# Token-major projections as products of 512 columns, and norms spread by transfers over DRAM

## The chip, the cores and the metric

The kernel runs on one core of one Trainium2 chip. The metric is the device time of one execution in microseconds (us); the kernel before takes 1825.83 us, the median of 3 runs (1825.49 to 1829.49).

## The reference

One inference step of an encoder layer. 2048 prompt tokens and 8 sample sequences of 16 tokens, each a row x of 1024, are RMS-normalised and multiplied by one weight matrix; the columns of the result feed three groups of heads, whose gated outputs go through an output projection.

```python
h = rms_norm(x, norm_g) @ w_in
fox_cols, rwkv_cols, mem_cols = jnp.split(h, [FOX_COLS, FOX_COLS + RWKV_COLS], axis=-1)
# fox: q, k (normalised per head of 64), v, forget gates; causal attention with a decay bias
# memory: q (normalised per head), attention into 256 memory tokens
# rwkv: r, k, v, decay, a, gate; per head and token
kk = k * ph(k_k)
kk = kk * lax.rsqrt(jnp.maximum(jnp.sum(kk * kk, axis=-1, keepdims=True), 1e-24))
S, y = rwkv_scan(s0, r, decay, k, v, kk, a)
mu = jnp.mean(y, axis=-1, keepdims=True)
var = jnp.mean(jnp.square(y - mu), axis=-1, keepdims=True)
yn = (y - mu) * lax.rsqrt(var + GN_EPS) * ph(gn_w) + ph(gn_b)
...
y = x + o @ w_out
```

Here rwkv has 6 heads of 64, fox 6 and memory 4. All is fp32. Two norms matter for the change: that of `kk` and that of `yn`, each one number per head and token, which then multiplies all 64 channels of the head.

## The kernel before

**Two stages.** The first stage (`p1`, to about 1130 us) normalises x, makes all projections and the whole rwkv group; what the attention needs goes to DRAM (`q_d`, `k_d`, `v_d`, `mq_d`, gates `fg_d`, `mg_d`, outputs `o_d`). The second stage (`p2`) does the attentions and the output projection. Buffers of the second stage lie where those of the first were, so a first buffer of `lt` (attention weights `P`, the raw output weights) is free only when the first stage's last user of that memory is done.

**Products in three parts.** The matrix engine takes fp32 data rounded to a shorter form (fp32r in the profile). x and each weight block are split into a high and a low part; a product is high x high + high x low + low x high. The contraction of 1024 goes in 8 blocks k of 128. x lies channel-major, `xk[k]` is 128 channels x (high, low) x up to 640 tokens. `wd_load` brings 256 weight columns into two tiles `hl` (4 blocks of k each, `[part, k, column]`): in the first of four iterations from the input, splitting them on ScalarE and GpSimd and keeping the split form in DRAM (`w_d`); in the other three from there, 1 MB at a time.

**Channel-major and token-major.** `proj_d` (tile `pjd`) makes channel-major results: the weights are stationary, 256, 384 or 512 tokens stream. `wide` (tile `pjt`) makes token-major results of 128 tokens x 256 columns: x is stationary and the weights stream, three products of 256 columns for each k. One PSUM tile `pjt` holds two token tiles side by side, 48 products. PSUM tiles `pjt`, `pjd` and a few others share the 3 buffers of `pj`. `put` then copies the pair of token tiles to SBUF on ScalarE (tile `qk`, 2 buffers), normalises the heads of q and k (square on ScalarE, sum on VectorE, power on GpSimd, multiply on VectorE, gain on GpSimd) and stores them. Five `wide` sets over 17 token tiles, and two sets over the two tiles of the memory, make 89 token tiles.

**rwkv.** Per iteration (512 prompt tokens) and pair of heads p: `rwkv_in` prepares, and solves small triangular systems, whose blocks go to DRAM and back (`ld`, `yt`, `xd`); `rwkv_mid` and `rwkv_scan` run the chunks; `rwkv_out` normalises and gates, and stores to `o_d`. The samples are three more such passes of 128 tokens. In `rwkv_in` and `rwkv_out`, `per_head` sums squares over a head's 64 channels with tiny products (tile `pss`) into `inv`, tokens on partitions, one column per head and tile of 128 tokens; then `spread` brings those numbers back to channel-major form, each repeated over 64 partitions: for each column one fp32 product, stationary the column repeated 64 times, streaming the identity (tile `spr`). VectorE multiplies straight from PSUM: into `ar[:, 0]` in `rwkv_in`, into `ysb` (tile `yd`) in `rwkv_out`.

**The order.** All DMAs are issued by SyncE (its queue is SPq). The program is emitted in a natural order; then `_arrange` re-orders all of it: `_Op` gives each instruction a cost, `_schedule` simulates the five engines with buffers and waits, 18 tries are made, and the try with the shortest simulated end becomes the order of every engine. An engine takes its instructions strictly in that order. For a DMA the planner has four terms: SyncE's own time, a lag to the transfer's begin (300 ns), the time on the wire, and a time to landing.

Of the kernel before, what the change touches and what calls it, by code (L numbers as in the profile page):

```python
# [9 lines left out]
F32 = mybir.dt.float32  # L10
# [7 lines left out]
KC = 8  # L18
# [33 lines left out]
def kernel(ctx: ExitStack, tc: tile.TileContext, I: dict, O: dict):  # L52
    nc = tc.nc
    V, S, G, PE, SY = nc.vector, nc.scalar, nc.gpsimd, nc.tensor, nc.sync
# [3 lines left out]
    def mm(out, lhsT, rhs, start=True, stop=True):  # L58
        PE.matmul(out, lhsT, rhs, start=start, stop=stop, skip_group_check=True)  # L59

    def tt(e, out, a, b, op):
        e.tensor_tensor(out=out, in0=a, in1=b, op=op)  # L62

    def stt(out, a, s, b, op0, op1):
        V.scalar_tensor_tensor(out=out, in0=a, scalar=s, in1=b, op0=op0, op1=op1)
# [9 lines left out]
    M, A_, SUB, MAX = ALU.mult, ALU.add, ALU.subtract, ALU.max  # L75
# [47 lines left out]
    with ExitStack() as p1:  # L123
# [48 lines left out]
        def wd_load(*parts, src="w_in"):  # L172


            where, n = [], 0
            for c0, w in parts:
                if where and where[-1][0] + where[-1][1] == c0:
                    where[-1][1] += w
                else:
                    where.append([c0, w, n])  # L180
                n += w
            key = (src, *parts)
            kept = split.get(key)
            if kept is None and src == "w_in":
                split[key] = dt(f"w{len(split)}_d", [256, 8 * n])
            hl = [[], []]
            for j, k0 in enumerate(range(0, KC, 4)):
                both = ws.tile([128, 2, 4, 256], F32R, tag="hl", name="w")
                flat = both.rearrange("p a k c -> p (a k c)")[:, :8 * n]
                hi, lo = (flat[:, 4 * n * a:4 * n * (a + 1)].rearrange("p (k c) -> p k c", c=n) for a in range(2))  # L190
                if kept is not None:
                    SY.dma_start(flat.bitcast(F32), kept[128 * j:128 * j + 128])
                else:
                    raw = ws.tile([128, 4, 256], F32, tag="w", name="wraw", bufs=WRAW)[:, :, :n]
                    for c0, w, o in where:
                        SY.dma_start(raw[:, :, o:o + w], I[src][128 * k0:128 * (k0 + 4), c0:c0 + w].rearrange("(k p) c -> p k c", p=128))
                    S.copy(hi, raw)  # L197
                    tt(G, lo, raw, hi.bitcast(F32), SUB)
                    if key in split:
                        SY.dma_start(split[key][128 * j:128 * j + 128], flat.bitcast(F32))  # L200
                hl[0].append(hi)
                hl[1].append(lo)
            return hl

        def proj_d(hl, c, m, xk, off, n):
# [132 lines left out]
        def at(h, a=0):  # L338

            return slice(64 * (h ^ a), 64 * (h ^ a) + 64)  # L340

        def per_head(sq, nt):

            pss = ps.tile([128, 512], F32, tag="ra", name="pss")
            for t in range(nt):
                for j in range(2):
                    mm(pss[64 * j:64 * j + 64, 2 * t:2 * t + 2], sq[:, 128 * t + 64 * j:128 * t + 64 * j + 64],
                       bones[:, 0:128:64].bitcast(F32))
            r = sm.tile([128, 8], F32, tag="inv", name="inv")[:, :2 * nt]
            V.tensor_copy(r, pss[:, :2 * nt])  # L350
            return r

        def spread(r, nt, pool, tag):

            out = pool.tile([128, 512], F32, tag=tag, name="spr")
            for t in range(nt):
                for h in range(2):
                    mm(out[at(h), 128 * t:128 * t + 128], r[:, 2 * t + h:2 * t + h + 1].to_broadcast([128, 64]), ident)
            return out[:, :128 * nt]

        def rwkv_in(p, k, r, v, g, sample, tok0):

# [34 lines left out]
            V.tensor_copy(wc, wx[:, :, seg])  # L397

            stt(seg3(ar[:, 0, :n]), seg3(k), col(NKK), wx[:, :, 0:seg], M, M)
            tt(V, ar[:, 0, :n], ar[:, 0, :n], spread(inv, nt, ps, "ra"), M)  # L400
            tt(V, seg3(ar[:, 1, :n]), seg3(r), wx[:, :, 1:seg + 1], M)

            ts(G, e5, e3, col(HKA), col(OHKA), M, A_)
# [233 lines left out]
        def rwkv_out(p, sample, n, nch, tok0, gt, bv, py, so):  # L637

            nt = n // 128
            two = rv.tile([128, 2, 512], F32, tag="bt", name="yd")  # L640
            ysb, sq = two[:, 0, :n], two[:, 1, :n]
            S.copy(ysb, py.rearrange("p c t -> p (c t)")[:, :n])
            yc = pg.tile([128, 512], F32, tag="gr", bufs=2, name="yc")[:, :n]
            mm(yc, centre, ysb)
            S.activation(sq, yc, AF.Square)
            S.copy(ysb, yc)
            r = per_head(sq, nt)
            rsqrt_small(r, r, 2 * nt, 1.0 / 64, GN_EPS)
            stt(ysb, ysb, vh[:, GW5 + p:GW5 + p + 1], spread(r, nt, ps, "ra"), M, M)
            stt(bv, bv, vh[:, GB5 + p:GB5 + p + 1], ysb, A_, A_)  # L650
            tt(V, bv, bv, gt, M)
            SY.dma_start(o_d[384 + 128 * p:384 + 128 * (p + 1), tok0:tok0 + n], bv)
            if sample:
                for c in range(2):
                    pt = pg.tile([128, 512], F32, tag="gr", bufs=2, name="pst")
                    for s in range(4):
                        PE.transpose(pt[0:64, 128 * s:128 * s + 128], so[:, c, s, :], ident)
                    sst = rv.tile([64, 4, 2, 64], F32, tag="gm", name="sst", bufs=2)
                    S.copy(sst, pt[0:64, :].rearrange("p (s h k) -> p s h k", h=2, k=64))
                    for h in range(2):  # L660
                        SY.dma_start(O["rs_s"][4 * c:4 * c + 4, 2 * p + h].rearrange("s v k -> v s k"), sst[:, :, h, :])
# [39 lines left out]
                tt(G, o_[:, :, n * j:n * j + n], s4[:, :, n * j:n * j + n],  # L701
                   GAIN[w].unsqueeze(1).unsqueeze(1).to_broadcast([128, nt, n, 64]), M)

        def put(out, parts, t0):

            nt, n = out.shape[1], len(parts)
            o_ = sm.tile([128, 512], F32, tag="qk", name="qk")[:, :128 * nt * n].rearrange("p (t c) -> p t c", t=nt)
            h4 = lambda ap: ap.rearrange("p t (h d) -> p t h d", d=64)
            whats = [w for w, _ in parts]
            S.copy(o_, out)  # L710
            n = sum(GAIN[w] is not None for w in whats)
            if n:
                normed(h4(o_[:, :, :128 * n]), whats[:n])
            spans_ = [(0, 2, parts[0])] if len(parts) == 2 and parts[1] == (whats[0], parts[0][1] + 128) else [
                (j, 1, x) for j, x in enumerate(parts)]
            for j, m, (w, c) in spans_:
                for dst in targets(w, t0, nt):
                    SY.dma_start(dst[:, :, c:c + 128 * m], o_[:, :, 128 * j:128 * (j + m)])
# [5 lines left out]
        def wide(parts, xk, nt, t0):  # L724
            hl = wd_load(*columns(parts), src="w_mem" if parts[0][0] in "KV" else "w_in")
            for a in range(0, nt, 2):
                m = min(2, nt - a)
                out = pj.tile([128, 2, 256], F32, tag="pj", name="pjt")
                for t in range(m):
                    ts_ = slice(128 * (a + t), 128 * (a + t) + 128)  # L730
                    for k in range(KC):
                        for x, y in ((0, 0), (0, 1), (1, 0)):
                            mm(out[:, t], xk[k][:, x, ts_], hl[y][k // 4][:, k % 4],
                               start=k == 0 and x + y == 0, stop=k == KC - 1 and x == 1)
                put(out[:, :m], parts, 16 if a == 4 else t0 + a)

        def narrow(hl, c, part, xk, blocks, tok0):

# [6 lines left out]
        def turn(sb, off, nb, part, tok0):  # L745
            pt = pj.tile([128, 512], F32, tag="pj", name="ptok")
            for t in range(nb // 128):
                PE.transpose(pt[:, 128 * t:128 * t + 128], sb[:, 128 * t:128 * t + 128], ident)
            for a, m, r0 in spans(tok0, off, nb):
                put(pt[:, a:a + m].rearrange("p (t c) -> p t c", c=128), [part], r0 // 128)  # L750

        def gate(hl, c, dst, xk, blocks, tok0):
            for off, nb in blocks:
# [179 lines left out]
    with ExitStack() as p2:  # L933
# [497 lines left out]
        at, mix = 0, []  # L1431
# [112 lines left out]
class _Op:  # L1544


    def __init__(self, i, eng):
# [25 lines left out]
        if eng == "SP":  # L1573
            size = 4 * list(outs[0].ap)[0][1] * _free(list(outs[0].ap))
            run = min(4 * list(a.ap)[-1][1] if list(a.ap)[-1][0] == 1 else 4 for a in aps)
            self.own, self.wire = (430 if run < 512 else 360), size / 230
            self.time = 1300 + (size / 140 - size / 230) * (run < 1024) / 2
            return
        wide = sum(k > 1 and "SB" in space(a) for k, a in zip(sizes, ins))
        self.reads = wide > 0  # L1580
# [201 lines left out]
def _schedule(p, rank, stay, loose=()):  # L1782
# [33 lines left out]
    while len(order) < count:  # L1816
# [37 lines left out]
        c = cost[nodes[x][0]]  # L1854
        if e == "SP":
            free[e] = s + c.own
            wire = max(wire, s + c.own + 300) + c.wire
            end[x] = wire + c.time
        elif e == "PE":
            for j, k in enumerate(nodes[x]):  # L1860
# [168 lines left out]
```

## Time and profile before

| | |
|---|---|
| median of 3 runs | 1825.83 us (1825.49 to 1829.49) |
| profiled execution, its own time | 1826.43 us |
| its span | 1824.6 us |
| TensorE matmul (PE) busy | 1756.1 us, 96% |
| VectorE (DVE), ScalarE (ACT), GpSimd (POOL) busy | 927.2, 895.5, 793.7 us |
| mean granted TensorE clock | 0.967 |

The profile names a group of instructions by the tile written, the tiles read (for a matmul the streaming one first, then the stationary one), its shape and its count. The two times of a timeline row are the start and the length of a run of like instructions, in us from the span's start. A matmul's recorded duration has a fixed tail that overlaps the next one; how fast they follow is read from the length of a run over its count. In the waits, the first column is who waited, then for whom, the total, the times, the longest.

### The profile page before, as it was taken

What the parts mean: (1) busy time and instruction counts of PE and PEld (TensorE: products, weight loads), DVE (VectorE), ACT (ScalarE), POOL (GpSimd) and SP (SyncE); (2) the same over time, 40 slices, a digit from 0 to 9 for tenths busy, and PEclk for the clock granted to TensorE, in tenths of its full rate; (3) what the DMA queues carried; (4) which work ended last, traced back from release to release, by engine and by line L of the source; (5) the groups of instructions that cost most, each with busy time, mean ns of one, the idle gap of its engine ahead of it and who ended that gap; (6) DMA issues with size and microseconds to landing.
All of it is one profiled execution on the core that took longest, in us unless ns stands there. A gap on an engine that the chain in (4) does not pass through costs nothing.

```text
span 1824.6 us, 41978 instructions
## 1 busy us (share of the span) xinstructions
PE 1756.1 (96%) x16883; PEld 1395.2 (76%) x16883; DVE 927.2 (51%) x2102; ACT 895.5 (49%) x1755; POOL 793.7 (43%) x818
## 2 busy tenths in 40 slices
PE   7999999999999999998999998999999999999998
PEld 6998999788877888876788886666666566667776
DVE  5544444464445553545743453767455545575213
ACT  5424343524234323324332434887888477986452
POOL 4555342242131341311332152567676265876452
PEclk8999999999999999999999999899999589999999
DMA  6767463745446464535363353434437542354422
GB/s 193 242 206 242 138 203 113 240 164 174 139 153 203 148 220 163 161 102 178 108 220 131 124 156 120 155 117 156 152 124 242 181 160 87 124 174 145 159 99 97
DMA packets 208905, 292.42 MB, mean 160 GB/s; under 512 B 56844, under 2 KB 161790, under 8 KB 192838
## 3 DMA queue, kind: packets, MB, share of 16 engines
q1 hardware_dynamic: 208710, 289.73, 48.5%
q8 instruction: 133, 2.18, 0.5%
q14 instruction: 62, 0.51, 0.1%
HBM read 202.58 MB, written 87.08 MB: 159 GB/s over the span
## 4 chain that ended last, share of the span: by engine, by line
PE 79%; DVE 7%; ACT 5%; DMA 3%; issue 3%; SPq 1%; POOL 1%; DVEq 0%; ACTq 0%; POOLq 0%
PE pjd L59 20%; PE pjt L59 12%; PE py L59 10%; PE po L59 9%; PE pS L59 7%; PE pm L59 4%; PE sc L59 2%; PE sy L59 1%; PE gr L59 1%; PE pz L59 1%; PE pa L59 1%; PE spr L59 1%; DMA w<-w_d 1%; PE gw L59 1%; PE gx L59 1%
## 5 line engine op out<-in xcount | busy, mean ns | idle before, releaser
L59 PE MATMUL pjd<-xk,w 128*128 128x512 f32 (+4 forms) x2280 | 522.6, 373 | 8.9 <-DVE xk L62 4.1
L59 PEld LDWEIGHTS pjd<-xk,w 128*128 128x128 f32 (+1 forms) x2280 | 380.4, 190 | 75.6 <-issue 10.2
L62 POOL TENSOR_TENSOR Pl<-P,Ph 128x512 fp32r<-128x512 f32 (+3 forms) x272 | 315.4, 1170 | 158.5 <-ACT Ph L1137 122.2
L59 PE MATMUL pjt<-w,xk 128*128 128x256 f32 x2040 | 282.4, 290 | 6.8 <-issue 3.5
L59 PEld LDWEIGHTS pjt<-w,xk 128*128 128x128 f32 x2040 | 260.1, 193 | 16.0 <-issue 7.8
L59 PE MATMUL py<-W,oh 128*128 128x512 f32 x816 | 248.7, 404 | 1.4 <-DVE rb L1179 1.4
L1134 ACT ACTIVATE P<-pS,NB 128x512 f32<-128x512 f32 x240 | 148.7, 623 | 70.8 <-PE pS L59 48.6
L59 PEld LDWEIGHTS py<-W,oh 128*128 128x128 f32 x816 | 150.1, 189 | 40.3 <-DVE rb L1179 1.8
L1078 DVE TENSOR_REDUCE mx<-pm 128x1 f32<-128x512 f32 (+2 forms) x240 | 140.8, 605 | 63.5 <-PE pm L59 60.7
L59 PE MATMUL pS<-Q,K 128*128 128x512 f32 (+1 forms) x480 | 162.6, 397 | 7.8 <-ACT P L1134 3.2
L1137 ACT CAST Ph<-P 128x512 fp32r<-128x512 f32 (+3 forms) x272 | 151.8, 564 | 18.6 <-PE po L59 13.7
L59 PE MATMUL po<-Ph,vt 128*65 128x512 f32 x480 | 156.8, 380 | 0.9 <-ACT ob L1157 0.5
L62 DVE TENSOR_TENSOR xo<-py,xo 128x512 f32<-128x512 f32 x68 | 46.7, 687 | 154.6 <-PE py L59 154.6
L59 PEld LDWEIGHTS pS<-Q,K 128*128 128x128 f32 (+1 forms) x480 | 88.7, 197 | 40.2 <-ACT P L1134 14.0
L62 POOL TENSOR_TENSOR nr<-nr,mhalf 128x8 f32<-128x8 f32 (+2 forms) x43 | 60.9, 1416 | 115.5 <-DVE nr L68 102.0
L59 PE MATMUL pm<-K,Q 67*128 67x512 f32 (+2 forms) x240 | 97.8, 424 | 2.8 <-DVE mx L1078 2.1
L62 POOL TENSOR_TENSOR w<-wraw,w 128x1024 fp32r<-128x1024 f32 (+1 forms) x34 | 79.8, 2348 | 43.8 <-ACT w L197 43.4
L59 PE MATMUL po<-Pl,vt 128*65 128x512 f32 x240 | 90.5, 377 | 0.2
L59 PEld LDWEIGHTS po<-Ph,vt 128*65 128x65 f32 x480 | 64.5, 142 | 26.5 <-issue 3.0
L710 ACT COPY qk<-pjt 128x512 f32<-128x512 f32 (+1 forms) x47 | 26.2, 565 | 102.5 <-PE pjt L59 63.3
L62 POOL TENSOR_TENSOR oh<-ot,oh 128x384 fp32r<-128x384 f32 (+2 forms) x38 | 45.9, 1207 | 61.6 <-ACT oh L1340 51.0
L59 PEld LDWEIGHTS pm<-K,Q 67*128 67x128 f32 x240 | 49.4, 209 | 20.3 <-DVE mx L1078 8.3
(399 smaller groups left out, 2847.4 us busy)
## 6 DMA issues: line engine op xcount, KB each, us to landing
w<-w_d SPq DMA_DIRECT2D x84, 1024.0 KB
w_d<-w SPq DMA_DIRECT2D x28, 1024.0 KB
y_d<-xo SPq DMA_DIRECT2D x21, 512.0 KB
wraw<-in_w_in SPq DMA_DIRECT2D x36, 256.0 KB
xo<-in_x SPq DMA_DIRECT2D x17, 512.0 KB
xo<-y_d SPq DMA_DIRECT2D x17, 512.0 KB
xt<-in_x SPq DMA_DIRECT2D x24, 256.0 KB
xraw<-in_xT SPq DMA_DIRECT2D x24, 256.0 KB
```

What stands on the lines that cost most here:

```text
L59: PE.matmul(out, lhsT, rhs, start=start, stop=stop, skip_group_check=True)
L62: e.tensor_tensor(out=out, in0=a, in1=b, op=op)
L710: S.copy(o_, out)
L1078: V.tensor_reduce(out=q["mx"][:, h, t, c0 // 512:c0 // 512 + 1], in_=pm[:, :n], op=MAX, axis=AX.X)
L1134: S.activation(P_[:, c0:], pS[:, c0:], AF.Exp, bias=NB[:, qb, 2 * hp + h, kt:kt + 1] if fox else 0.0)
L1137: S.copy(Ph[:, c0:], P_[:, c0:])
```

## The change

Three edits.

`wide`: the PSUM tile `pjt` now belongs to one token tile. Its two halves of 256 columns take different sums: x's high part times the weights' high and low part, streamed together as 512 columns, fills both; x's low part times the weights' high part adds to the first half. ScalarE copies the first half into `qk`, VectorE adds the second half to it. `put` gets the finished `qk`.

`spread`: the numbers of `inv` are transposed by one product to 8 rows of 128 (`spt`), copied to SBUF on ScalarE, written to a DRAM buffer `sp_d` (4 KB, 4 buffers), and two DMAs read them back, each repeating one head's 512 numbers over 64 partitions of a given SBUF tile. In `rwkv_in` that tile is `ar[:, 1]`, which until then held the squares and afterwards takes r times the decay; in `rwkv_out` it is the tile that held the squares (`sq`). `per_head` orders its columns by head first, for that.

The planner's DMA terms: wire speed, lag and landing time get other numbers.

```diff
@@ wd_load
-            hl = [[], []]
+            hl = [[], [], []]
...
+                hl[2].append(flat.rearrange("p (a k c) -> p a k c", a=2, k=4))
@@ per_head
-                    mm(pss[64 * j:64 * j + 64, 2 * t:2 * t + 2], sq[:, 128 * t + 64 * j:128 * t + 64 * j + 64],
+                    mm(pss[64 * j:64 * j + 64, t:t + nt + 1:nt], sq[:, 128 * t + 64 * j:128 * t + 64 * j + 64],
                        bones[:, 0:128:64].bitcast(F32))
@@ spread
-        def spread(r, nt, pool, tag):
-            out = pool.tile([128, 512], F32, tag=tag, name="spr")
-            for t in range(nt):
-                for h in range(2):
-                    mm(out[at(h), 128 * t:128 * t + 128], r[:, 2 * t + h:2 * t + h + 1].to_broadcast([128, 64]), ident)
-            return out[:, :128 * nt]
+        def spread(out, r, nt):
+            n = 2 * nt
+            pt = ps.tile([128, 512], F32, tag="ra", name="spt")
+            PE.transpose(pt[0:n, 0:128], r, ident)
+            rr = sm.tile([8, 128], F32, tag="spr", name="spr", bufs=1)[:n]
+            S.copy(rr, pt[0:n, 0:128])
+            sp_d = dt("sp_d", [8, 128], bufs=4)
+            SY.dma_start(sp_d[:n], rr)
+            for h in range(2):
+                SY.dma_start(out[at(h)], sp_d[nt * h:nt * h + nt].rearrange("t p -> (t p)").partition_broadcast(64))
@@ rwkv_in
-            tt(V, ar[:, 0, :n], ar[:, 0, :n], spread(inv, nt, ps, "ra"), M)
+            spread(ar[:, 1, :n], inv, nt)
+            tt(V, ar[:, 0, :n], ar[:, 0, :n], ar[:, 1, :n], M)
@@ rwkv_out
-            stt(ysb, ysb, vh[:, GW5 + p:GW5 + p + 1], spread(r, nt, ps, "ra"), M, M)
+            spread(sq, r, nt)
+            stt(ysb, ysb, vh[:, GW5 + p:GW5 + p + 1], sq, M, M)
@@ put, wide (narrow calls tokens and S.copy itself, as put did)
+        def tokens(nt, n):
+            return sm.tile([128, 512], F32, tag="qk", name="qk")[:, :128 * nt * n].rearrange("p (t c) -> p t c", t=nt)
...
-                out = pj.tile([128, 2, 256], F32, tag="pj", name="pjt")
+                o_ = tokens(m, 2)
                 for t in range(m):
+                    out = pj.tile([128, 2, 256], F32, tag="pj", name="pjt")
                     ts_ = slice(128 * (a + t), 128 * (a + t) + 128)
                     for k in range(KC):
-                        for x, y in ((0, 0), (0, 1), (1, 0)):
-                            mm(out[:, t], xk[k][:, x, ts_], hl[y][k // 4][:, k % 4],
-                               start=k == 0 and x + y == 0, stop=k == KC - 1 and x == 1)
-                put(out[:, :m], parts, 16 if a == 4 else t0 + a)
+                        mm(out, xk[k][:, 0, ts_], hl[2][k // 4][:, :, k % 4], start=k == 0, stop=False)
+                        mm(out[:, 0], xk[k][:, 1, ts_], hl[0][k // 4][:, k % 4], start=False, stop=k == KC - 1)
+                    S.copy(o_[:, t], out[:, 0])
+                    tt(V, o_[:, t], out[:, 1], o_[:, t], A_)
+                put(o_, parts, 16 if a == 4 else t0 + a)
@@ _Op, _schedule (planner, DMAs only)
-            self.own, self.wire = (430 if run < 512 else 360), size / 230
-            self.time = 1300 + (size / 140 - size / 230) * (run < 1024) / 2
+            self.own, self.wire = (430 if run < 512 else 360), size / (270 if run < 1024 else 340)
+            self.time = 700
...
-            wire = max(wire, s + c.own + 300) + c.wire
+            wire = max(wire, s + c.own + 600) + c.wire
```

More of the change, by code (lines that the diff above doesn't have):

```diff
@@ L702, in normed, with put @@
                    GAIN[w].unsqueeze(1).unsqueeze(1).to_broadcast([128, nt, n, 64]), M)
-        def put(out, parts, t0):
-            nt, n = out.shape[1], len(parts)
-            o_ = sm.tile([128, 512], F32, tag="qk", name="qk")[:, :128 * nt * n].rearrange("p (t c) -> p t c", t=nt)
+        def tokens(nt, n):
+            return sm.tile([128, 512], F32, tag="qk", name="qk")[:, :128 * nt * n].rearrange("p (t c) -> p t c", t=nt)
+        def put(o_, parts, t0):
+            nt, n = o_.shape[1], len(parts)
             h4 = lambda ap: ap.rearrange("p t (h d) -> p t h d", d=64)
             whats = [w for w, _ in parts]
-            S.copy(o_, out)
             n = sum(GAIN[w] is not None for w in whats)
@@ L749, in turn @@
             for a, m, r0 in spans(tok0, off, nb):
-                put(pt[:, a:a + m].rearrange("p (t c) -> p t c", c=128), [part], r0 // 128)
+                o_ = tokens(m // 128, 1)
+                S.copy(o_, pt[:, a:a + m].rearrange("p (t c) -> p t c", c=128))
+                put(o_, [part], r0 // 128)
         def gate(hl, c, dst, xk, blocks, tok0):
```

## The prediction

> **What bounds the kernel now.** I read the page first: its span and the busy shares, then the chain of work that ended last.
>
> ```profile
> span 1824.6 us, 41978 instructions
> PE 1756.1 (96%) x16883; PEld 1395.2 (76%) x16883; DVE 927.2 (51%) x2102; ACT 895.5 (49%) x1755; POOL 793.7 (43%) x818
> PE 79%; DVE 7%; ACT 5%; DMA 3%; issue 3%; SPq 1%; POOL 1%; DVEq 0%; ACTq 0%; POOLq 0%
> ```
>
> TensorE is busy 96% of the span and is 79% of the chain. Next, busy time by stage (columns: PE, weight loads, DVE, ACT, POOL, then granted clock, DMA share, GB/s).
>
> ```profile
> 60.00:1130.00 1070.00, 1040.43 (x13071) 890.18 (x13069) 530.33 (x1376) 381.22 (x794) 348.08 (x379) 0.99 0.51 165
> 1130.00:1170.00 40.00, 31.18 (x146) 21.55 (x147) 33.76 (x60) 30.27 (x59) 18.03 (x24) 0.74 0.61 189
> 1400.00:1480.00 80.00, 74.50 (x414) 47.95 (x412) 45.59 (x108) 43.98 (x88) 30.75 (x36) 0.68 0.57 190
> ```
>
> The change's arithmetic lies in the first row: PE 1040 of 1070 us at clock 0.99, DVE half busy, ACT 36%. There, PE time removed is span removed as long as the others keep up; 29.6 us are idle already. The two other rows are where the clock is lost: the change of stage, and 80 us of sample attention.
>
> **Spread leaves TensorE.** The groups by shape, then TensorE's timeline around a prompt block, a sample block, and a comparable transpose:
>
> ```profile
> L59 PE MATMUL spr<-ident,inv 128*64 128x128 f32 x408 | 28.9, 280 | 0.0
> ...
> 214.13 0.28 PE L59 MATMUL pjt<-w,xk 128*128 128x256 f32 x1
> 214.34 1.09 PE L59 MATMUL spr<-ident,inv 128*64 128x128 f32 x16
> 215.36 0.97 PE L59 MATMUL pjd<-xk,w 128*128 128x384 f32 x4
> ...
> 293.45 0.44 PE L59 MATMUL spr<-ident,inv 128*64 128x128 f32 x4
> 293.82 1.46 PE L59 MATMUL pjd<-xk,w 128*128 128x256 f32 x10
> ...
> 1055.17 0.36 PE L59 MATMUL pjt<-w,xk 128*128 128x256 f32 x1
> 1055.37 0.27 PE L853 MATMUL psh<-ident,sho 128*9 128x128 f32 x1
> 1055.40 0.36 PE L59 MATMUL pjt<-w,xk 128*128 128x256 f32 x1
> ```
>
> A block of 16 holds the array from 214.34 to 215.36, 1.02 us. The product before it started 0.21 earlier, where 0.12 is its pace (next part), so entering the block costs another 0.09. 408 records are 24 blocks of 16 and 6 of 4: 24 x 1.11 + 6 x (0.37 + 0.09) = 29.4 us. In exchange come 30 transposes of 8 (or 2) columns. The nearest row is `psh`, 9 columns: with it between two pjt products they stand 0.23 apart instead of 0.12, so 0.11 each, 3.3 us. **Net -26.1 us.**
>
> **The product of 512.** TensorE's pace is read from long unbroken runs in the chain (start, length, count); the second, in the third iteration, is 512 wide.
>
> ```profile
> 647.94 13.44 PE pjt L59 x112
> 756.44 6.39 PE pjd L59 x28
> 738.34 4.63 PE pjd L59 x20
> L59 PE MATMUL pjt<-w,xk 128*128 128x256 f32 x2040 | 282.4, 290 | 6.8 <-issue 3.5 <-ACT qk L710 3.2
> L59 PE MATMUL pjt<-w,xm 128*128 128x256 f32 x96 | 13.4, 287 | 0.0
> ```
>
> 256 columns take 13.44 / 112 = 120 ns, 512 take 6.39 / 28 = 228 ns (231 in the slower run). Twice the columns is not twice the time: 12 ns of each product do not depend on its columns. The change streams the same 768 columns per k in two products instead of three: 3 x 120 - (228 + 120) = 12 ns. 2040 + 96 records are 24 for each of 89 token tiles, so 89 x 8 x 12 = **8.4 us less** (6 with 231; 0 if a streamed pair of halves paid the 12 ns twice). The Trainium skill, "TensorE: Matmul & The Clock Gate", Back-to-back issue gap, gives a warm product N/2.4 + 2.5 ns, which is 109 and 216 ns. By it this edit would bring 2.5 ns per k, an estimated 1.8 us, and the sum would end 6.6 us higher; both runs measured here are 11 to 12 ns above it, so I keep the rows.
>
> **What the wide edit adds elsewhere.**
>
> ```profile
> L710 ACT COPY qk<-pjt x47: 373/587/603, 85.6 to 1106.4; 128x512 f32<-128x512 f32 x42, 128x256 f32<-128x256 f32 x5
> L601 DVE COPY su<-pz 64x256 f32<-64x256 f32 x24 | 9.2, 424 | 16.2 <-ACT su L601 16.0
> ```
>
> ACT: 89 copies of 256 at 0.373 instead of 42 at 0.587 and 5 at 0.373, +6.7 us. DVE: 89 additions from PSUM; the nearest 256-column read of PSUM is 0.424, so +38 us, 53% busy instead of 50% in this stage. Both are covered by TensorE; without that cover they would lengthen the drain of a tile from 0.59 to 0.80 us. What is not covered is room. The three `pj` banks held 3 x 5.8 us of pjt work, now 3 x 2.8, while `qk` keeps 2 buffers and its long way through five engines and a store. PE and its weight loads waited for pjt some 6.7 us in this stage (the 3.5 and 3.2 that end the pjt group row above). With half the run-ahead I double that: **+6.7**, between 0 (the planner puts channel-major products there) and 13.
>
> **What spread adds.** Rows of the chain for short transfers, issue to landing, the issue of a repeating read, a copy of 9 rows, and the consumer:
>
> ```profile
> 309.04 1.65 DMA xd<-ld
> 823.93 2.45 DMA ld<-yt
> L1193 SPq DMA_DIRECT2D rb<-rd x38: 450/528/1522, 1179.3 to 1718.2; - x38
> L855 ACT COPY shr<-psh x4: 237/576/577, 1056.1 to 1063.6; 9x512 f32<-9x512 f32 x3, 9x128 f32<-9x128 f32 x1
> 74.94 0.68 DVE L62 TENSOR_TENSOR AR<-AR,spr 128x512 f32<-128x512 f32 x1
> 70.43 1.09 PE L59 MATMUL spr<-ident,inv 128*64 128x128 f32 x16
> ```
>
> Latency: transpose 0.27, copy 0.24, write 1.8, first read's issue 0.53, second read to landing some 2.0 (between 1.65 and 2.45): 4.8 us, where spr took 1.1. In `rwkv_in` the block starts 4.5 us before its consumer, since the scan and exponentials are in between, so little is late. r times decay now queues behind that consumer (it overwrites the spread numbers), 0.7 us for the `gr` products, which PE fills with projections. In `rwkv_out` only the gated output waits, and it goes to DRAM; taken as 0 while projections remain.
>
> At the end of the stage none remain:
>
> ```profile
> 1128.22 1.09 PE L59 MATMUL spr<-ident,inv 128*64 128x128 f32 x16
> 1130.20 0.74 DVE L65 SCALAR_TENSOR_TENSOR yd<-yd,vh,spr 128x512 f32<-128x512 f32 x1
> 1132.80 0.62 SPq L652 DMA_DIRECT2D o_d<-bv  x1
> 1137.34 0.33 SPq L970 DMA_DIRECT2D cl<-in_clf  x1
> ```
>
> The last block runs when PE has nothing else, so its 1.1 us are no gain: **+1.1**. The multiply moves from 1130.2 to about 1128.2 + 4.8 = 1133.0, and with it the store and the buffers that `cl` takes: **+3.0**, between 0 (attention starts in other memory) and 5 (at the 0.74 clock of this stretch a gap costs more than itself).
>
> SyncE's queue gets 30 x 3 issues, 30 x (0.36 + 2 x 0.53) = 43 us, and each reading pair stands behind its own write's landing, 1.3 us after that issue. Behind it wait weight loads and stores. I take 0 on the path, for the loads come early:
>
> ```profile
> SPq L192 <- PE pjd L59: 104.7, 45, 7.9
> ```
>
> SyncE waits 105 us for PE's channel-major products to free a weight buffer before a load (L192), so the loads are ahead of need. The other end is priced as a rival below.
>
> **Planner.** The new terms price an 8 KB hop at 0.43 + 0.60 + 0.03 + 0.70 = 1.76 us (before 2.07; the row says 1.65) and a 1 MB weight load at 0.36 + 0.60 + 3.08 + 0.70 = 4.74 (before 6.5). The row for that load:
>
> ```profile
> 689.51 5.41 DMA w<-w_d
> ```
>
> So hops are better priced, large loads 0.7 us too short. The whole order is made anew, second stage included. I take 0; the bound is half of what the sample stretch loses today, 80 x 0.32 + 5.5 = 31 us, so 15 either way.
>
> **Sum**, against the profiled execution's own 1826.4 (1824.6 of span and 1.8 around it, 0.6 above the median): 1826.4 - 26.1 - 8.4 + 6.7 + 1.1 + 3.0 = 1802.7, forecast **1803 us**; with the small terms' bounds 1794 to 1812.
>
> **Rivals.**
>
> *The 512 product saves nothing* (the switch is paid per 256 columns): 1803 + 8.4 = 1811. Against it: pjd's 512, whose stream is one piece, shows one switch. For it: here the stream is two pieces, 1024 numbers apart. 10%.
>
> *The rwkv chain takes over.* With 3% less to hide behind, the chain through DVE, POOL and DRAM sets the end of some passes, and half of what remains beyond the waits comes back, 14 us: 1817 (1812 to 1825). For it: the chain already holds 7% DVE and 3% DMA; against it, PE's own waits in this stage are small, the largest of this kind being
>
> ```profile
> PE gx L59 <- issue: 6.1, 5, 1.9
> PE gx L59 <- ACT g L488: 3.2, 3, 2.1
> ```
>
> 14%.
>
> *The new order helps*: better-priced hops shorten the sample stretch by the 15 us: 1788 (1776 to 1794). 15%.
>
> *Slower: SyncE's queue holds up weight loads.* It has happened once:
>
> ```profile
> 689.93 5.31 SPq L456 DMA_DIRECT2D xd<-ld  x8
> 696.37 0.53 SPq L192 DMA_DIRECT2D w<-w_d  x1
> 705.66 1.86 PE L59 MATMUL pjt<-w,xk 128*128 128x256 f32 x7 [2.97 <-issue]
> 700.00:720.00 20.00, 17.03 (x365) 15.50 (x360) 2.84 (x5) 7.51 (x16) 1.08 (x3) 0.83 0.44 148
> ```
>
> Eight hops that wait for a write keep the queue for 5.3 us, the weight load behind them leaves at 696.4, and PE stands 2.97 us for it; then 20 us run at clock 0.83, another 3.4 us. One such event costs 6.4 us. (The Trainium skill, "TensorE: Matmul & The Clock Gate", Part 1, says that an idle window of about 3.4 us puts the clock to half; the dip in the last row agrees.) A spread now is such a hop 30 times over, in the first stage, and the planner believes weight loads shorter than they are. Four events give 1803 + 4 x 6.4 = 1828.6 and undo the gain; with five it is 1835 (1826 to 1845). For it: this event; against it: the 105 us of waiting for buffers, and that reads take 2 issues where this took 8. 18%.
>
> **How the numbers follow.** Forecast 43%, the useless 512 product 10%, the rwkv chain 14%, the helpful order 15%, the queue 18%. 0.2%, about what a measurement of this kernel tells from no change, is 3.7 us: 1822.2 to 1829.5 around 1825.8. Faster: 43 + 10 + 15, and 11 of the chain's 14, 79%; same: 3 of the chain and 3 of the queue, 6%; slower: the queue's other 15%. The range 1782 to 1828 leaves out the lower third of the helpful order (5%) and the queue's time above it (15%); the likeliest case's own range is 1794 to 1812.
>
> **What would show it.** Right: no `spr` matmuls, 30 short transposes and PE busy near 1722 us; pjt runs at 348 ns for each pair of products; PE idle between 60 us and the end of the first stage at 30 to 45 us; that end some 30 us earlier, near 1103. Wrong: pairs at 360 ns (512 product); PE waiting in long pieces for weights with SyncE at `sp_d` just before (queue), for `gr`, `gw`, `gx` (chain), or for pjt's banks beyond 13 us; the second stage, from its first attention product to the end, longer or shorter than before by over 5 us (order).

## The result, and the profile after

| | before | after |
|---|---|---|
| median of 6 runs, us | 1826.0 (1820.4 to 1830.9) | 1815.0 (1808.7 to 1819.8) |
| ratio, 95% interval | | 0.9931 (0.9908 to 0.9953) |
| profiled execution, us | 1826.4 | 1808.7 |
| first stage, to the first attention product, us | 1137.7 | 1137.6 |
| second stage, us | 686.9 | 669.4 |

The change is a gain of 0.7%, 11 to 13 us, about half of what was forecast. The six runs of either kernel lie 10 to 11 us apart, and the profiled execution of after is the fastest of its six, so a stage's length from one profile is good to some 6 us, and to 9 at worst (the terms alone, below).

The page of after, its span, busy shares and the three groups of the token-major product:

```profile
span 1807.0 us, 40189 instructions
PE 1710.3 (95%) x15793; PEld 1324.7 (73%) x15793; DVE 958.7 (53%) x2191; ACT 903.6 (50%) x1827; POOL 799.4 (44%) x818
...
L59 PE MATMUL pjt<-w,xk 128*128 128x512 f32 (+1 forms) x1360 | 281.9, 349 | 7.9 <-DVE qk L62 7.7
...
L744 ACT COPY qk<-pjt 128x256 f32<-128x256 f32 x89 | 31.7, 374 | 123.9 <-PE pjt L59 98.9
...
L62 DVE TENSOR_TENSOR qk<-pjt,qk 128x256 f32<-128x256 f32 x89 | 36.3, 417 | 49.6 <-ACT qk L744 45.6
```

Busy time by stage, split at the first attention product (columns as before: PE, weight loads, DVE, ACT, POOL, granted clock, DMA share, GB/s). First the kernel before:

```profile
0.00:1137.70 1137.70, 1091.87 (x13329) 935.90 (x13329) 569.67 (x1458) 419.65 (x880) 380.18 (x424) 0.98 0.52 169
1137.70:1824.60 686.90, 664.20 (x3554) 459.29 (x3554) 357.51 (x644) 475.81 (x875) 413.50 (x394) 0.94 0.44 145
```

The same split of the kernel after, and three of its stretches:

```profile
0.00:1137.60 1137.60, 1062.97 (x12239) 872.17 (x12239) 602.58 (x1542) 429.52 (x951) 382.48 (x419) 0.98 0.54 174
1137.60:1807.00 669.40, 647.36 (x3554) 452.53 (x3554) 356.16 (x649) 474.05 (x877) 416.96 (x400) 0.96 0.46 150
...
60.00:1130.00 1070.00, 1016.51 (x12035) 831.53 (x12033) 565.04 (x1462) 391.03 (x863) 350.51 (x371) 0.99 0.52 171
1130.00:1170.00 40.00, 30.10 (x119) 20.03 (x120) 33.94 (x61) 29.28 (x59) 20.84 (x31) 0.63 0.61 187
1400.00:1480.00 80.00, 75.41 (x629) 52.99 (x628) 55.16 (x125) 59.92 (x119) 45.12 (x53) 0.96 0.71 240
```

This is the puzzle. In the first stage, where both edits of the arithmetic lie, TensorE is busy 28.9 us less (1091.9 to 1063.0) and the stage ends at the same time: its idle time grew from 45.8 to 74.6 us. The second stage, which neither of them touches, is 17.5 us shorter. There the same 3554 products take 664.2 us before and 647.4 after, at a mean clock of 0.94 and 0.96; in the sample stretch, 1400 to 1480 us, the clock is 0.96 where it was 0.68. Only the order of the work is different there: every one of the three edits has it made anew, and the planner's DMA terms also re-price it. The traces keep the stretches in which TensorE was granted half its clock. Added up, they are 79.4 us of before's second stage and 48.2 of after's; what half of the difference gives, 15.6 us, is nearly all of the 16.8 by which the products got shorter.

Who kept TensorE waiting in the first stage of after (waits of PE; then of SyncE's queue; then of VectorE, up to 1150 us):

```profile
PE gw L59 <- DVE x L475: 8.7, 7, 1.9
PE pjt L59 <- DVE qk L62: 7.7, 2, 7.5
PE pn L843 <- DVE ncn L68: 5.5, 1, 5.5
PE pjd L59 <- DVE xsk L65: 4.9, 1, 4.9
```

```profile
SPq L362 <- ACT spr L360: 100.0, 20, 14.3
SPq L192 <- PE pjd L59: 92.1, 42, 7.7
...
SPq L364 <- DMA sp_d<-spr: 31.3, 22, 6.3
```

```profile
DVE x L475 <- DMA xd<-ld: 27.0, 8, 6.7
DVE yd L65 <- DMA yd<-sp_d: 19.0, 13, 5.8
DVE AR L62 <- DMA AR<-sp_d: 16.3, 10, 2.8
```

The waits of before that answer to the first row of PE and the first of VectorE (L469 of before is L475 of after):

```profile
PE gw L59 <- DVE x L469: 1.3, 4, 0.5
DVE x L469 <- DMA xd<-ld: 1.3, 2, 0.9
```

Before, VectorE waited for the hops of the triangular solve 1.3 us in all, twice. Now it is 27.0 us, and 35.3 us more for the spread's reads. TensorE's extra idle time has no single owner: its four waits shown for after are 26.8 us, where before had 1.3 us for `x`, 3.2 for `qk` and none for the two others. One of the waits for a hop in the timeline of after, and how it gets to TensorE:

```profile
945.88 4.15 SPq L462 DMA_DIRECT2D xd<-ld  x8
...
951.39 0.45 DVE L475 STREAM_TRANSPOSE x<-xd 128x256 f32<-128x256 f32 x1 [6.04 <-DMA xd<-ld]
...
951.89 0.75 PE L59 MATMUL gw<-x,gm 32*32 32x32 f32 x64 [1.54 <-DVE x L475]
```

Eight issues take 4.15 us, VectorE stands 6.04 us until the last has landed, and of that TensorE loses 1.54: the rest it fills with projections.

### The profile page after: what moved, and what is told of

The parts are those of the page before. It is cut to its first block, busy times and chain, and to the rows that moved or that the text cites. A ratio compares the mean times of both kernels' runs of the same rounds, so it can differ in the third digit from the quotient of the medians.

```text
span 1807.0 us, 40189 instructions
## 1 busy us (share of the span) xinstructions
PE 1710.3 (95%) x15793; PEld 1324.7 (73%) x15793; DVE 958.7 (53%) x2191; ACT 903.6 (50%) x1827; POOL 799.4 (44%) x818
## 5 line engine op out<-in xcount | busy, mean ns | idle before, releaser
L59 PE MATMUL pjd<-xk,w 128*128 128x512 f32 (+4 forms) x2280 | 530.0, 375 | 21.6 <-DVE xsk L65 4.9
L59 PEld LDWEIGHTS pjd<-xk,w 128*128 128x128 f32 (+1 forms) x2280 | 384.9, 190 | 91.9 <-issue 8.6
L59 PE MATMUL pjt<-w,xk 128*128 128x512 f32 (+1 forms) x1360 | 281.9, 349 | 7.9 <-DVE qk L62 7.7
L59 PEld LDWEIGHTS pjt<-w,xk 128*128 128x128 f32 x1360 | 214.6, 190 | 42.1 <-DVE qk L62 8.4
L59 PE MATMUL py<-W,oh 128*128 128x512 f32 x816 | 242.2, 401 | 1.4 <-DVE rb L1192 1.4
L59 PE MATMUL pS<-Q,K 128*128 128x512 f32 (+2 forms) x480 | 157.4, 391 | 3.2 <-ACT P L1147 2.4
L744 ACT COPY qk<-pjt 128x256 f32<-128x256 f32 x89 | 31.7, 374 | 123.9 <-PE pjt L59 98.9
L62 DVE TENSOR_TENSOR qk<-pjt,qk 128x256 f32<-128x256 f32 x89 | 36.3, 417 | 49.6 <-ACT qk L744 45.6
```

The costliest lines, as they stand in the source:

```text
L744: S.copy(o_[:, t], out[:, 0])
```

## The experiments

Two theories to begin with. **A**: the edits' gain is lost in the first stage because the rwkv chain sets its end; the terms did nothing but shorten the second stage. **B**: the terms price hops too short and lengthen the first stage; the edits' gain is there, but covered. Every kernel computes the reference in full. All numbers in one table, for the text below; a stage's PE column is its busy time. The ratios are against runs of before made beside each set, whose median was 1825.8 to 1827.6 us.

| kernel | median | ratio (95%) | profiled | stage 1 | PE | stage 2 | PE |
|---|---|---|---|---|---|---|---|
| before | 1826.0 | | 1826.4 | 1137.7 | 1091.9 | 686.9 | 664.2 |
| after | 1815.0 | 0.9931 (0.9908, 0.9953) | 1808.7 | 1137.6 | 1063.0 | 669.4 | 647.4 |
| terms alone | 1826.9 | 0.9987 (0.9968, 1.0006) | 1818.2 | 1154.7 | 1096.1 | 661.7 | 644.0 |
| both edits, old terms | 1879.1 | 1.0297 (1.0268, 1.0325) | 1887.9 | 1177.5 | 1097.5 | 708.6 | 672.9 |
| spread, old terms | 1894.7 | 1.0374 (1.0338, 1.0410) | 1886.7 | 1187.9 | 1087.7 | 697.0 | 668.2 |
| 512 product, old terms | 1853.6 | 1.0150 (1.0124, 1.0175) | 1855.5 | 1162.4 | 1104.0 | 691.3 | 663.6 |
| 512 product, new terms | 1821.1 | 0.9976 (0.9960, 0.9993) | 1822.5 | 1160.9 | 1091.6 | 659.8 | 642.1 |
| spread, new terms | 1813.5 | 0.9926 (0.9901, 0.9951) | 1814.5 | 1136.1 | 1072.6 | 676.6 | 654.5 |
| before, other tries | 1813.4 | 0.9933 (0.9914, 0.9952) | 1813.9 | 1112.2 | 1087.0 | 699.9 | 667.3 |
| after, other tries | 1820.8 | 0.9970 (0.9953, 0.9986) | 1820.1 | 1149.3 | 1071.9 | 669.0 | 650.8 |
| after, longer hops | 1806.4 | 0.9883 (0.9855, 0.9912) | 1809.6 | 1127.6 | 1066.0 | 680.2 | 655.2 |
| terms alone, longer hops | 1828.2 | 0.9996 (0.9971, 1.0021) | 1828.1 | 1150.3 | 1099.6 | 676.0 | 654.0 |
| after, longer hops, other tries | 1799.1 | 0.9844 (0.9818, 0.9869) | 1799.1 | 1129.5 | 1065.4 | 667.8 | 649.2 |
| terms alone, longer hops, other tries | 1825.3 | 0.9988 (0.9969, 1.0008) | 1824.0 | 1154.5 | 1097.2 | 667.7 | 647.8 |

**The terms alone, and both edits with the old terms.** The first is the kernel before with only this, the second the kernel after with only this undone:

```diff
-            self.own, self.wire = (430 if run < 512 else 360), size / 230
-            self.time = 1300 + (size / 140 - size / 230) * (run < 1024) / 2
+            self.own, self.wire = (430 if run < 512 else 360), size / (270 if run < 1024 else 340)
+            self.time = 700
...
-            wire = max(wire, s + c.own + 300) + c.wire
+            wire = max(wire, s + c.own + 600) + c.wire
```

> The kernel before with the planner's new DMA terms alone; the arithmetic is untouched. Theory A (the saving of the two edits is lost because the first stage is bound by its chain of small steps and hops, and what was gained came from the new order in the second stage): first attention product at 1135 to 1140 us as before, second stage some 15 us shorter, time 1809 to 1816. Theory B (the new terms price hops too short, their users are ordered too early and TensorE stands for them): PE idle in the first stage rises from 39 to 55 us or more, first attention product at 1150 or later, time 1825 to 1835. Theory C (the order is a lottery, any new order moves either stage by 10 us or so): no number, but then neither stage follows A or B.

> Both edits (product of 512, spread by transfers) with the planner's old DMA terms. Theory A: first attention product still near 1137 us, PE busy in the first stage 33 us less and PE idle 30 us more, time 1820 to 1830. Theory B: first attention product near 1105 to 1112, time 1795 to 1802.

Terms alone, by stage, and its waits of PE and of VectorE:

```profile
0.00:1154.70 1154.70, 1096.06 (x13329) 936.32 (x13329) 576.72 (x1457) 418.74 (x880) 384.21 (x424) 0.98 0.51 167
1154.70:1816.40 661.70, 643.96 (x3554) 446.80 (x3554) 349.70 (x645) 475.46 (x876) 410.20 (x394) 0.97 0.46 151
```

```profile
PE gw L59 <- DVE x L469: 10.4, 8, 2.3
```

```profile
DVE x L469 <- DMA xd<-ld: 24.2, 10, 4.6
```

The terms move both stages and leave the time: the first is 17.0 us longer, the second 25.2 shorter (8.7 of the difference is this profiled execution, that much under its median), and the median is that of before, 0.9987. A falls here: the first stage does not stay at 1138 without the edits. B's three figures came: 58.6 us idle in the first stage, the first attention product at 1154.7, and 1826.9. The waits for `x` that I saw in after, 8.7 us on TensorE and 27.0 on VectorE, are here without either edit of the arithmetic, so they do not need those; nor do they need the new terms, for both edits with the old terms have 5.8 and 11.5 us of them. Against the same terms the edits do shorten the first stage, from 1154.7 to 1137.6: 17.1 of the 33.1 us by which TensorE's busy time shrinks.

Both edits with the old terms, by stage:

```profile
0.00:1177.50 1177.50, 1097.50 (x12236) 894.54 (x12236) 596.70 (x1542) 427.50 (x948) 381.05 (x419) 0.95 0.52 169
1177.50:1886.10 708.60, 672.85 (x3558) 466.63 (x3558) 364.06 (x649) 479.88 (x880) 413.56 (x400) 0.93 0.43 142
```

B would have this kernel the fastest, and A had 1820 to 1830; it is 53 us slower than before, so neither foresaw it. The first stage has after's products (12236 records, after 12239) and takes TensorE 1097.5 us for them instead of 1063.0: the clock is 0.95, and 80 us are idle. The trace has 119.5 us of this stage at half clock, that of after 48.4; half of the difference, 35.6 us, is the whole of the 34.5. The edits need other terms than the old ones, or these gave a bad order.

**Each edit alone, under either terms.** Spread only is after with `wide` and `put` as before; the 512 product only is after with `spread`, `per_head` and their two callers as before. Each was run with the old terms and with the new.

```diff
# 512 product alone: the spread of before
-            spread(ar[:, 1, :n], inv, nt)
-            tt(V, ar[:, 0, :n], ar[:, 0, :n], ar[:, 1, :n], M)
+            tt(V, ar[:, 0, :n], ar[:, 0, :n], spread(inv, nt, ps, "ra"), M)
# spread alone: the products of before
-                        mm(out, xk[k][:, 0, ts_], hl[2][k // 4][:, :, k % 4], start=k == 0, stop=False)
-                        mm(out[:, 0], xk[k][:, 1, ts_], hl[0][k // 4][:, k % 4], start=False, stop=k == KC - 1)
+                        for x, y in ((0, 0), (0, 1), (1, 0)):
+                            mm(out[:, t], xk[k][:, x, ts_], hl[y][k // 4][:, k % 4],
+                               start=k == 0 and x + y == 0, stop=k == KC - 1 and x == 1)
```

> Spread by transfers alone, old products, old terms. If spread's hops and its place in SyncE's queue eat its own 26 us, the time is 1822 to 1832 and PE idle in the first stage is 60 us or more; if they do not, the first attention product comes at 1113 to 1118 and the time is 1800 to 1808.

> The product of 512 with one PSUM tile for each token tile alone, old spread, old terms. If the halved room of the PSUM tiles eats the 7 us that the pace gives, the time is 1824 to 1834 with PE waiting for pjt and pjd on the qk copies and additions; if it does not, 1817 to 1820.

> The product of 512 with the planner's new terms, old spread. Beside the terms alone (ratio 0.9987). If the parts add up under the new terms, this edit's 7 us off TensorE show: ratio 0.994 to 0.997, some 1815 to 1821. If the outcome is ruled by how each new order happens to fall (theory C), it lies anywhere from 0.985 to 1.015.

> Spread by transfers with the planner's new terms, old products. If the parts add up: 26 us off TensorE, less the 30 us of idle time that the changed kernel has: ratio 0.993 to 1.000. If spread itself makes the first stage longer whatever the terms, as with the old ones (1.037): 1.02 to 1.04. Under theory C anywhere from 0.985 to 1.02.

With the old terms each edit alone makes the kernel slower, by 3.7% and 1.5%, far above both ranges that I had written for either. The spread kernel holds a single wait of 14.7 us at the end of the solve:

```profile
PE gw L59 <- DVE x L474: 26.4, 5, 14.7
```

With the new terms both are faster than before, spread by 0.7%, just past its range for parts that add up, and the 512 product by 0.2%, short of its. Against the terms alone spread gives 0.6% (0.9926 / 0.9987), the 512 product 0.1%, which is not clear of noise, and both together 0.6%. Spread's first stage is 18.6 us shorter than that of the terms alone, where 22 were predicted (26.1 - 1.1 - 3.0); the 512 product's is 6.2 longer, where it should have been 1.7 shorter (8.4 - 6.7). So the order that comes with an edit can weigh as much as the edit's work.

**How much is the order itself?** A third theory, **C**: an order is a draw, and what separates two kernels is partly luck. The program and the costs stay, and only the weights shift with which the planner makes its 18 tries:

```diff
-_TRIES = ((0.3, 0), (0.45, 0), (0.6, 0))
+_TRIES = ((0.25, 0), (0.4, 0), (0.55, 0))
```

> The kernel before, with nothing changed but the three weights of the planner's tries (0.3, 0.45, 0.6 become 0.25, 0.4, 0.55): the same instructions and costs, another order. Theory C: the time moves by 10 us or more, most likely up, 1835 to 1870, and the half-clock time moves with it. Theories A and B: within 5 us of 1826.

> The changed kernel with the same shift of the tries' weights. Theory C: moves by 10 us or more, either way, 1800 to 1850. Theories A and B: within 5 us of 1814.

The kernel before with other tries, by stage:

```profile
0.00:1112.20 1112.20, 1086.98 (x13310) 932.26 (x13310) 564.75 (x1453) 417.95 (x878) 373.81 (x418) 0.99 0.52 173
1112.20:1812.10 699.90, 667.31 (x3573) 464.97 (x3573) 360.67 (x650) 474.55 (x878) 416.43 (x400) 0.94 0.43 144
```

Nothing but other tries makes the kernel before 12.6 us faster, as much as the whole change does, and the changed kernel 5.8 us slower; between these two the change is a loss of 7 us. C had 10 us or more, most likely up: the size came for one kernel, the way down was not foreseen, and 5.8 lies between C's figure and the 5 of A and B. A gain of 0.7% is thus no larger than one draw of the order. What looks like more than a draw is the second stage: over five orders with the old terms it takes 686.9 to 708.6 us, mean 696.7; over nine with the new wire terms 659.8 to 680.2, mean 669.8. The groups are 27 us apart and do not overlap, though between the nearest two the gap of 6.7 is no more than one profile's error. The first stage of the kernel without edits goes the other way: 1137.7 and 1112.2 with the old terms, 1150.3, 1154.5 and 1154.7 with the new.

**A price for hops.** Theory **D**: the new 700 ns from the wire's end to landing are right for 1 MB and too few for a hop, so the planner puts the hop's consumer too early. Transfers of up to 128 KB get their old 1300 back, in the kernel after and in that with the terms alone, each with the first tries and with the other ones:

```diff
-            self.time = 700
+            self.time = 700 if size > 131072 else 1300
```

> The changed kernel; of the planner's new terms, the time to landing of transfers up to 128 KB is put back from 700 to 1300 ns, the wire speeds and the lag stay. Theory D (the new terms shorten the second stage by pricing large transfers well, and lengthen the first by pricing hops 0.6 us or more too short, so that their users stand at the head of in-order engines): TensorE's wait for gw falls from 8.7 us to under 3, the first attention product comes at 1110 to 1125 instead of 1137.6, the second stage stays at 660 to 675, time 1785 to 1800. Theory C (lottery): anywhere from 1800 to 1835, gw as it falls.

> The kernel before (old products, old spread) with the same terms as the run before this one. Theory D: against the terms alone (first attention product at 1154.7, second stage 662), the first stage ends 20 to 35 us earlier, 1120 to 1135, the second stage stays at 660 to 670, time 1790 to 1805; what the two edits are worth under well-priced hops is the difference to the changed kernel with these terms, 15 to 30 us if TensorE is the bound, 5 or less if it is not.

> The changed kernel with hops at 1300 ns and the tries' weights shifted (0.25, 0.4, 0.55): a second draw of the order. Theory D: again gw waits under 3 us and 1785 to 1800. Theory C: 1800 to 1835, unlike its twin.

> The kernel before with hops at 1300 ns, new wire speeds and lag, and the tries' weights shifted: a second draw. Theory D: within 8 us of its twin, 1790 to 1810, and above the changed kernel's second draw. Theory C: 1800 to 1835, in either order with the changed kernel's.

The kernel after with longer hops, its waits of VectorE up to 1150 us and of PE in the first stage:

```profile
DVE x L475 <- DMA xd<-ld: 16.0, 6, 5.8
DVE AR L62 <- DMA AR<-sp_d: 6.2, 5, 2.8
DVE yd L65 <- DMA yd<-sp_d: 2.5, 2, 1.5
```

```profile
PE gw L59 <- DVE x L475: 2.9, 4, 1.0
```

And the fastest kernel, with other tries beside it, by stage:

```profile
0.00:1129.50 1129.50, 1065.36 (x12244) 877.49 (x12244) 605.77 (x1544) 430.02 (x953) 387.71 (x424) 0.98 0.54 176
1129.50:1797.30 667.80, 649.23 (x3550) 452.27 (x3550) 362.75 (x648) 472.71 (x875) 412.05 (x395) 0.96 0.45 150
```

For the kernel with edits the time goes D's way: 8.6 us less with the first tries (1815.0 to 1806.4), 21.7 with the other (1820.8 to 1799.1). VectorE's waits for the spread's reads fall from 35.3 us to 8.7, and with the other tries from 32.5 to 16.1; TensorE's for `x` fall from 8.7 to 2.9, and from 13.4 to 4.3. D's figures came only in part: with the first tries `gw` is under 3 us, but the first attention product at 1127.6, the second stage of 680.2 and the 1806.4 all lie above their ranges; with the other tries 1799.1 lies inside D's and just outside C's, and `gw` is over 3. 1799.1 us, 0.9844 (0.9818 to 0.9869) of before, beats both kernels. For the kernel without edits D fails: 1828.2 and 1825.3, no gain at all, though its waits for `x` fall too (10.4 to 5.1 and 3.0), and the first stage stays at 1150.3 and 1154.5. So the price of hops seems to matter where the spread's hops are, and is not what lengthens the first stage under the new terms. That it is the price and not two lucky orders is likely, not shown: a draw alone moved the time by up to 12.6 us, and one of the two gains is smaller than that.

With the hops priced, the edits are worth 21.8 us (1828.2 to 1806.4) and 26.2 (1825.3 to 1799.1): two pairs of orders, both near the 23 that the prediction gave them. With the new terms as they were it was 11.9 (1826.9 to 1815.0), and with the old ones a loss of 53.

## Why the prediction was right or wrong

**Spread leaves TensorE, and the 512 product: right.** TensorE's work in the first stage fell by 33.1 us against the same terms (1096.1 to 1063.0), predicted 34.5. Under the new terms, with and without the other edit, spread takes 28.6 and 23.5 us off it, the 512 product 9.6 and 4.5, where 26.1 and 8.4 were predicted. The pace of the new pair, read from TensorE's timeline (a run is named by the shape it begins with; 512 and 256 alternate in it):

```profile
94.38 14.52 PE L59 MATMUL pjt<-w,xk 128*128 128x256 f32 x82
```

82 products are 41 pairs; less some 0.2 us of tail, 14.3 / 41 = 349 ns a pair, predicted 348, before 360. So the switch is paid once per 512, and the rival that denied this falls. By the formula for an isolated product in the Trainium skill, "TensorE: Matmul & The Clock Gate", Back-to-back issue gap, the pair would take an estimated 325 ns (768 columns and two gaps); the trace does not agree, 349. That PE's 1710.3 in all lies 11 us under the 1722 foreseen is not the edits' doing: the second stage, where the forecast had no change, is busy 16.8 us less, and the first, against before, 5.6 us more than foreseen.

**The transposes: right.** 0.11 us each was foreseen, from `psh`. A place in the timeline of after where single products stand around one:

```profile
713.97 0.27 PE L358 MATMUL spt<-ident,inv 128*8 128x128 f32 x1
714.00 0.36 PE L59 MATMUL pjt<-w,xk 128*128 128x256 f32 x1
714.20 0.40 PE L59 MATMUL pjd<-xk,w 128*128 128x512 f32 x1
```

The next product starts 0.03 us behind the transpose, but then holds TensorE 0.20 us, where 256 columns take 0.12. That is the 0.11 foreseen: most of a transpose's cost shows in the product behind it.

**Room for pjt: right in its place, and in its size by luck.** TensorE's products into `pjt` wait 7.7 us for `qk` (3.2 before), those into `pjd`, which share its buffers, 3.2 (0.6 before): 7.1 us more in all, predicted 6.7 more. The 6.7 was a doubling of 6.7 us of waits, of which 3.5 are put down to "issue", that is to nothing that the profile shows, and not to room. And what came is nearly one event, in the first iteration:

```profile
115.09 0.92 ACT L744 COPY qk<-pjt 128x256 f32<-128x256 f32 x3 [5.70 <-DMA q_d<-qk]
...
116.91 7.16 PE L59 MATMUL pjt<-w,xk 128*128 128x512 f32 x32 [7.55 <-DVE qk L62]
...
116.91:124.07 7.16, 7.16 (x32) 5.97 (x32) 3.80 (x15) 2.06 (x4) 3.08 (x3) 0.79 0.12 34
```

ScalarE's copy waits 5.70 us for a store to leave one of the two `qk` buffers; then the three PSUM tiles are full, and TensorE stands 7.55 us. The 16 pairs after it take 7.16 us at a granted clock of 0.79 (the last row is that stretch), some 435 ns each instead of 349, another 1.4 us. (The Trainium skill, "TensorE: Matmul & The Clock Gate", Part 1, puts the clock to half after an idle window of about 3.4 us; this row agrees with it.) So long a wait is not needed: in the kernel before, the wait of 2.97 us that the prediction shows was followed by 6.8 us at clock 0.50. A single wait of 7.3 to 8.7 us for `qk` is in every kernel with the 512 product and the new terms.

**End of the stage: 3.0 foreseen, not seen.** The last transpose starts at 1130.5, and its reads go out at 1135.8 and 1136.8, later than I had feared; yet the first attention product starts at 1137.6 and waits for its own `Q`, not for them. That `Q` comes from transposes (`pt`) which stood 2.66 us for a read of `q_d`:

```profile
1130.52 0.27 PE L358 MATMUL spt<-ident,inv 128*8 128x128 f32 x1 [0.63 <-POOL inv L62]
...
1135.81 1.12 PE L1011 MATMUL pt<-ident,tok 128*128 128x128 f32 x4 [2.66 <-DMA tok<-q_d]
...
1136.80 0.47 SPq L364 DMA_DIRECT2D yd<-sp_d  x1
...
1137.64 0.45 PE L59 MATMUL pm<-K,Q 67*128 67x128 f32 x1 [0.71 <-ACT Q L1077]
```

**SyncE's queue taken as 0: right; the slower rival did not come.** SyncE still waits 92.1 us for TensorE to free weight buffers (before 104.7), so weight loads are still ahead, and TensorE waited for a weight load once, 0.9 us. But the queue does stand for the spread: 100 us for its copy, 31 for its write's landing. With weights on time, what it can have held up is hops and stores; that it made them late is argued, not shown.

**The step that failed is the planner: "So hops are better priced ... I take 0; the bound is ... 15 either way".** The time of 1815 lies in the range of 1782 to 1828, but not by the path of the sum, and that is luck. The sum takes its 23 us out of the first stage, which ended where it did before (1137.7 and 1137.6); what was gained, 17.5 us, lies in the second stage, where the sum had 0. Three things were wrong in the step. The size: in one profile each, the terms moved the two stages of the kernel without edits by 17 and 25 us, not by 15 at most, in opposite directions, and the two happened to cancel (0.9987), so that the sum's 0 looked right. The price: 1.76 us for a hop of 8 KB alone agreed with its row, and I did not carry it on to the hops that the edit itself adds; priced higher, VectorE's waits for the spread's reads fell by 27 and 16 us, and the kernel with edits gained 9 and 22. And the draw: I had no term for an order made anew, and other tries alone are worth 3 to 13 us in four pairs (12.6, 5.8, 7.3, 2.9). The own range of 1794 to 1812 was too narrow for that, and missed 1815 by 3; the wide one held it.

The list of signs worked better than the sum, and says that the path was another. It asked for the first stage's end near 1103 (1137.6 came), for 30 to 45 us idle between 60 us and that end (1077.6 - (1062.97 - 43.93) = 58.6 came; 43.93 is what PE does in the first 60 us), and named a second stage changed by over 5 us as the sign of the order (17.5).

**The rivals.** The helpful order came true where I looked for it, the sample stretch at clock 0.96, and was paid for in the first stage. The rwkv chain forecast 1817, near what came, but hardly by its mechanism: TensorE's waits before `gr`, `gw` and `gx` add up to 15.2 us in after and 13.3 before, so the chain did not take over; with the hops priced, the same chain leaves room for 1799.

**Open.** Which of the terms, wire or lag, lengthens the first stage was not run. Nor is it shown why the edits' orders under the old terms are that bad: the half clock in their first stage (119.5 us with both edits, 113.1 with spread alone) is most of the loss there, but what brings it, many short waits beside the one of 14.7 us with spread alone or something else, is open. The hop price rests on two pairs of orders, where a draw alone moves up to 13 us; the signs agree, the size is not settled, and a third order could turn it.

## What to carry to other kernels

Where a planner re-orders the whole program, a change of its costs is a change of the kernel: give it its own line in the forecast, and measure it alone. A transfer that an edit adds should be priced for the planner as it is measured; otherwise the edit's gain can go to waits of others, as it seems to have done here. Before a gain of under 1% is credited to an edit, shift something that should not matter, and see how far the time moves.

## What the runs showed that I had not expected

What tells the second stages apart is the clock more than the idle time. The products are the same in all 14 kernels (3550 to 3573 records, as a few change sides at the split), but they take from 642 us (512 product, new terms) to 673 (both edits, old terms). The half-clock time that the traces keep, 33.6 to 99.1 us a stage, follows that with a correlation of 0.98, and each us of it goes with 0.49 us more of busy time. Idle time follows it less well (0.91), and before and after have the same, 22.7 and 22.0 us, with 16.8 us between their busy times. A wait is not even needed for the clock to fall. In the kernel after:

```profile
1434.00:1437.40 3.40, 3.40 (x120) 3.38 (x117) 1.42 (x2) 1.58 (x3) 2.87 (x3) 1.00 0.38 82
1437.40:1444.20 6.80, 6.80 (x30) 5.22 (x26) 3.82 (x9) 3.53 (x7) 2.70 (x3) 0.50 0.82 277
```

In the first row TensorE is busy throughout, with products of 16 columns (`po<-sD,sA`) of the sample attention; in the 6.8 us that follow it has half its clock. Why was not tested. Of the 27 us that lie between the means of the old terms and the new in the second stage, 17.8 are busy time and 9.1 idle time, and 34.8 us less at half clock are enough for the former; what in the order spares it is open.

The spread's reads of 128 KB, each repeating 2 KB over 64 partitions, take longer than the 2.0 us that I took from hops of 8 KB: these rows of the chain of waits, of after with longer hops and of the same with other tries, show 2.75 and 6.19 us, the second from the issue of the first of two reads.

```profile
755.00 2.75 DMA yd<-sp_d
```

```profile
218.97 6.19 DMA yd<-sp_d
```
